# Where the GLA's low-rank decay keeps its temporaries: arena slots, or the mLSTM's second state tile and the LRU weights' tile

## The chip, the cores and the metric

One core of one Trainium2 chip runs the whole program once per launch. The metric is device microseconds per execution. Five engines work beside each other, each in its own order: TensorE (PE, with its weight loads PEld), VectorE (DVE), ScalarE (ACT), GpSimd (POOL) and SyncE (SP), which issues the DMAs. All data is float32; a matmul with float32 accuracy is made of three passes over operands that were split into a high and a low part.

## The reference, cut to what matters

One decoder layer over 2048 tokens of width 1024: a norm, one input projection, four token mixers side by side (RG-LRU, mLSTM, HGRN2, GLA), each times a gate path and projected, merged by sigmoid gates, and an output projection. HGRN2 and GLA are the same recurrence with different decays:

```python
def step(state, xs):                      # gla_chunkwise, per chunk
    G = jnp.cumsum(gc, axis=2)
    diff = jnp.where(mask[:, :, None], G[:, :, :, None, :] - G[:, :, None, :, :], -jnp.inf)
    A = jnp.einsum('bhtd,bhsd,bhtsd->bhts', qc, kc, jnp.exp(diff))
    o = jnp.einsum('bhts,bhse->bhte', A, vc) + jnp.einsum('bhtd,bhde->bhte', qc * jnp.exp(G), state)
    ...
log_gk = jax.nn.log_sigmoid(g_lr @ g_w_lr2 + g_b_lr2) / GLA_GATE_TAU     # the low-rank decay, rank 16
og = gla_chunkwise(q, k, v, log_gk)
merged = jnp.sum(gates * proj, axis=2)    # four branches, in the order lru, mlstm, hgrn2, gla
```

## The kernel before, in words

The sequence is worked off in two halves of 1024 tokens; everything below happens once per half. Channels lie on the partitions, tokens on the free axis, in pieces of 512.

`ahead_pairs` makes most of the input projection, the LRU and the mLSTM. The mLSTM keeps its state in two tiles `self.C[0]` and `self.C[1]` (trace name `Cst`), read and written in turn; `self.lw` holds the LRU's block weights. Then comes `mixers`:

- `ip_vals(0..3)` makes the values of HGRN2 (0, 1) and GLA (2, 3) with TensorE; calls 2 and 3 also give the 16 columns `lrt` from which the decay is made (L1152, L1154, L1156 empty PSUM). Matmuls are line L284.
- Six rounds, called round 0 to round 5 here, of two `gla_tile`s each: round 0 and 1 are HGRN2 heads 0 and 1 (first and second 512 tokens), 2 and 3 are heads 2 and 3, 4 and 5 are the GLA's two pairs of heads. Each tile goes through a chain of small steps: scans L994 and L996 (from L995), exponents L999 to L1001, products L1002 and L1003, 32-wide matmuls L1019, four refinements L1038 to L1062, state and outputs L1075 to L1111, a norm L1121 to L1134, and a store of its output `y`.
- `load(r + 1)` loads the next round's inputs. In program order round 1 comes after `ip_vals(2)`, `ip_vals(3)`, `gla_decay()` and `load(2)`.
- `gla_decay` (L1189 to L1216) transposes `lrt` into `lt` (L1199, L1200), multiplies by the low-rank weights (L1206) and makes four decay tiles `g` of 512 tokens, each with one temporary `t`: Identity, Abs, Exp (L1208 to L1210), Ln (L231), then L1212 and L1213 on DVE. The decays are first read in rounds 4 and 5.
- `gates_ahead` makes the last six merge gates (matmuls L272).

`merge` then runs the four branches' projections (L272 again, 192 matmuls of 512 columns per branch) and multiplies each by its gate (L1331). Branches one and two take four fixed buffers (the two `gth` tiles and the two halves of `lw`), branches three and four take arena slots. Branch three needs rounds 0 to 3, branch four rounds 4 and 5.

Order of the work: the program is traced in order, then a scheduler places every instruction on its engine by a simulated timeline, the one with the lowest priority number first among those whose operands are ready. `mix()` lowers the number of `gla_decay` and of the tiles by 4000. So a later part may run ahead of an earlier one, unless it writes memory that the earlier one has still to read.

That memory is the `Arena`: 46 slots in `mixers`, 0 to 21 named `arena` in the trace, 22 to 29 `ma`, 30 to 45 `mb`. `get` takes the next free slot after the last one taken, and wraps; free and taken are counted in program order. At the start of `gla_decay` the turn stands at slot 22. With 27, 29 and 0 to 3 in use it gives: `lt` 22 and 23; `g` 24, 25 with `t` 26, 28; `g` 4, 5 with `t` 6, 7. `load(2)` gets 8 to 13, 22 and 23. Round 1 gets, first tile: `Gc` 26, `g8` 28, `d` 30, `wq` 31, `wk` 32; second tile: `Gc` 35, `g8` 36, `d` 37, `wq` 6, `wk` 7.

Of the kernel before, what the change touches and what calls it, by code (L numbers as in the profile page):

```python
# [145 lines left out]
class Trunk:  # L146
# [1043 lines left out]
    def gla_decay(self):  # L1190

        nc = self.nc
        V, A, T = nc.vector, nc.scalar, nc.tensor
        gs = []
        lt = self.F()
        for n in range(2):
            ps = self.pbank()
            for c in range(4):
                T.transpose(ps[0:16, c * 128:(c + 1) * 128], self.lrt[:, n * 4 + c, :], self.cs("id"))  # L1199
            V.tensor_copy(lt[0:16, n * 512:(n + 1) * 512], ps[0:16])  # L1200
        for p in range(2):
            gs.append([self.T(0, NU + 2 * NA if p else None) for _ in range(2)])
            for n in range(2):
                g, t = gs[p][n], self.T()
                ps = self.pbank()
                T.matmul(ps, self.wlr[:, p * 128:(p + 1) * 128], lt[0:16, n * 512:(n + 1) * 512], start=True, stop=True)  # L1206
                gg, tt = g[:, :512], t[:, :512]
                A.activation(gg, ps, AF.Identity, bias=self.pv("gb", p))  # L1208
                A.activation(tt, gg, AF.Abs)
                A.activation(tt, tt, AF.Exp, scale=-1.0)  # L1210
                self.ln(tt, tt, bias=1.0)
                V.scalar_tensor_tensor(gg, gg, 0.0, tt, op0=ALU.min, op1=ALU.subtract)  # L1212
                V.tensor_scalar(gg, gg, 1.0 / 16, None, op0=ALU.mult)  # L1213
                self.free(t)
        self.free(lt)
        return gs  # L1216


# [342 lines left out]
```

## Time and profile before

| | us |
|---|---|
| median of 3 runs (2855.47 to 2863.75) | 2856.83 |
| profiled execution | 2859.04 |
| its span from first to last instruction | 2857.0 |
| PE busy / weight loads busy | 2603.6 / 2149.5 |
| DVE, POOL, ACT busy | 1780.5, 1528.5, 1327.9 |

Busy times are averages over very different stages, so the stretches below are read one by one. "PEclk" is the TensorE clock that was granted, as a share of full speed. In a timeline the bracket at the end of a row is the engine's idle time before that row and what ended it.

### The profile page before, as it was taken

Reading aid. Unit: us, or ns where it says so; the run is one execution under the profiler, and the core shown is the slowest. Engines: PE = TensorE matmul, PEld = TensorE weight load, DVE = VectorE, ACT = ScalarE, POOL = GpSimd, SP = SyncE. Lnnn points to the kernel's source line nnn. Section 1 sums busy time; section 2 is a strip of 40 time slices with the busy share of each in tenths; the row PEclk is TensorE's granted clock in tenths of the full one; section 3 lists DMA queues with packets and bytes.
Section 4 is the critical chain, followed back from the end, with each engine's and each line's share of the span. In section 5 each row is a group of like instructions: output and inputs, shape, how many; then the busy total and the mean of one; then the engine's idle time right before and its main releaser. Section 6 shows DMA issues by size and latency. Waiting matters only on the chain. (4 is left out here: it accounts for less than half of the span.)

```text
span 2857.0 us, 45749 instructions
## 1 busy us (share of the span) xinstructions
PE 2603.6 (91%) x16800; PEld 2149.5 (75%) x16800; DVE 1780.5 (62%) x2907; ACT 1327.9 (46%) x2793; POOL 1528.5 (53%) x1273
## 2 busy tenths in 40 slices
PE   6999999999999977859999999997999998888699
PEld 4778778778889765648977778885888896676489
DVE  7686776877662777523476957757766618775241
ACT  5355444644432545562454445456344325445523
POOL 5566555444462766346475566553444627645563
PEclk9999999999999988779999999998999998989799
DMA  5133224454542465454432333244454424546631
GB/s 209 67 132 109 92 85 145 133 174 144 149 144 75 130 207 168 175 204 149 146 133 78 136 108 107 89 133 144 153 155 126 156 70 144 195 153 211 202 100 71
DMA packets 227071, 393.02 MB, mean 138 GB/s; under 512 B 20720, under 2 KB 78080, under 8 KB 226848
## 3 DMA queue, kind: packets, MB, share of 16 engines
q1 hardware_dynamic: 226848, 390.11, 41.4%
q8 instruction: 132, 2.16, 0.3%
q14 instruction: 91, 0.75, 0.1%
HBM read 270.42 MB, written 119.60 MB: 137 GB/s over the span
## 5 line engine op out<-in xcount | busy, mean ns | idle before, releaser
L422 POOL TENSOR_TENSOR wl<-wr,wh 128x512 fp32r<-128x512 f32 x264 | 370.4, 1408 | 314.4 <-ACT wh L421 285.9
L422 POOL TENSOR_TENSOR wl<-gth,wh 128x512 fp32r<-128x512 f32 x198 | 287.8, 1454 | 296.7 <-ACT wh L421 272.9
L254 POOL TENSOR_TENSOR wl<-wr,wh 128x512 fp32r<-128x512 f32 (+1 forms) x176 | 252.9, 1447 | 260.6 <-ACT wh L253 247.7
L427 PE MATMUL mx<-s,wh 128*128 128x512 f32 x1104 | 355.2, 400 | 19.9 <-POOL s L310 12.0
L272 PE MATMUL pb<-hh,wh 128*128 128x512 f32 x704 | 303.1, 432 | 38.3 <-DVE arena L1331 18.6
L427 PE MATMUL mx<-hh,wl 128*128 128x512 f32 x776 | 309.4, 399 | 6.4 <-POOL wl L422 6.4
L427 PE MATMUL mx<-hh,wh 128*128 128x512 f32 x776 | 308.8, 398 | 3.9 <-ACT wh L421 3.9
L427 PE MATMUL mx<-hl,wh 128*128 128x512 f32 x776 | 308.4, 397 | 0.0
L436 DVE TENSOR_TENSOR arena<-arena,mx 128x512 f32<-128x512 f32 x348 | 228.4, 680 | 121.6 <-PE mx L427 112.0
L272 PE MATMUL pb<-hl,wh 128*128 128x512 f32 x704 | 297.1, 422 | 2.5 <-DVE hl L1305 2.5
L272 PE MATMUL pb<-hh,wl 128*128 128x512 f32 x704 | 295.6, 420 | 0.0
L421 ACT ACTIVATE wh<-wr 128x512 fp32r<-128x512 f32 x264 | 164.1, 625 | 216.2 <-PE mx L427 126.5
L427 PEld LDWEIGHTS mx<-s,wh 128*128 128x128 f32 x1104 | 208.5, 190 | 73.5 <-POOL s L310 13.3
L284 PE MATMUL pb<-wl,hh 128*128 128x256 f32 (+1 forms) x880 | 250.5, 285 | 0.5 <-POOL wl L254 0.5
L284 PE MATMUL pb<-wh,hh 128*128 128x256 f32 (+1 forms) x880 | 249.8, 285 | 1.0 <-DVE ob L1366 1.0
L284 PE MATMUL pb<-wh,hl 128*128 128x256 f32 (+1 forms) x880 | 249.8, 284 | 0.0
L421 ACT ACTIVATE wh<-gth 128x512 fp32r<-128x512 f32 x198 | 124.1, 627 | 240.3 <-DVE gth L432 181.5
L427 PE MATMUL mx<-s,wl 128*128 128x512 f32 x552 | 218.0, 398 | 0.0
L272 PEld LDWEIGHTS pb<-hh,wh 128*128 128x128 f32 x704 | 143.3, 204 | 80.2 <-DVE arena L1331 20.4
L253 ACT ACTIVATE wh<-wr 128x512 fp32r<-128x512 f32 (+1 forms) x176 | 110.2, 628 | 151.2 <-PE pb L272 95.2
L427 PEld LDWEIGHTS mx<-hh,wl 128*128 128x128 f32 x776 | 146.7, 189 | 44.4 <-POOL wl L422 11.4
L427 PEld LDWEIGHTS mx<-hh,wh 128*128 128x128 f32 x776 | 147.4, 190 | 39.7 <-ACT wh L421 5.2
(535 smaller groups left out, 6338.5 us busy)
## 6 DMA issues: line engine op xcount, KB each, us to landing
wr<-in_wc_dram SPq DMA_DIRECT2D x246, 256.0 KB, 2.8
g<-arena SPq DMA_DIRECT2D x52, 512.0 KB, 3.9
gth<-in_wc_dram SPq DMA_DIRECT2D x66, 256.0 KB, 2.7
wr<-in_wb_dram SPq DMA_DIRECT2D x64, 256.0 KB, 3.5
hl<-y SPq DMA_DIRECT2D x32, 512.0 KB, 6.1
arena<-g SPq DMA_DIRECT2D x56, 256.0 KB, 3.3
y<-arena SPq DMA_DIRECT2D x36, 256.0 KB, 3.9
arena<-in_xT_dram SPq DMA_DIRECT2D x32, 256.0 KB, 5.1
```

Of the source, the lines that this page charges most:

```text
L253: nc.scalar.activation(hi, raw, AF.Copy)
L254: nc.gpsimd.tensor_tensor(lo, raw, hi, op=ALU.subtract)
L272: nc.tensor.matmul(ps, w[:, ws], h[:, ts], start=(k == 0 and i == 0), stop=(k == nk - 1 and i == 2))
L284: self.nc.tensor.matmul(v, h[:, cs], w[:, ws], start=(first and i == 0), stop=(last and i == 2))
L421: A.activation(hi, w, AF.Copy)
L422: G.tensor_tensor(lo, w, hi, op=ALU.subtract)
L427: nc.tensor.matmul(ps, wp[:, ws], xp, start=(k == 0 and i == 0), stop=(k == 3 and i == 2))
L436: V.tensor_tensor(o, x, y, op=ALU.add)
```

## The change

`gla_decay` no longer takes slots for `lt` and `t`. `lt` becomes the first 16 partitions of `self.lw`, and all four chains share the first 512 columns of `self.C[1]` as their one temporary. The four `g` still come from the arena.

```diff
-        lt = self.F()
+        lt = self.lw.rearrange("p a b -> p (a b)")
...
-                g, t = gs[p][n], self.T()
+                g = gs[p][n]
...
-                gg, tt = g[:, :512], t[:, :512]
+                gg, tt = g[:, :512], self.C[1][:, :512]
...
-                self.free(t)
-        self.free(lt)
         return gs
```

## Rows read from the trace of the kernel before

**Rows 1.** The page: busy time, share of the span and instructions of each engine.

```profile
PE 2603.6 (91%) x16800; PEld 2149.5 (75%) x16800; DVE 1780.5 (62%) x2907; ACT 1327.9 (46%) x2793; POOL 1528.5 (53%) x1273
```

**Rows 2.** Busy us per stretch, first half: PE, PEld, DVE, ACT, POOL; PEclk, DMA share, GB/s.

```profile
825.00:876.00 51.00, 46.17 (x574) 44.61 (x573) 37.12 (x62) 21.96 (x60) 30.95 (x32) 0.97 0.34 116
...
880.00:935.00 55.00, 54.58 (x448) 53.63 (x446) 7.81 (x36) 12.54 (x30) 14.25 (x12) 1.00 0.16 44
935.00:1003.00 68.00, 58.52 (x512) 45.74 (x510) 52.84 (x71) 39.97 (x92) 51.04 (x48) 0.92 0.47 152
1003.00:1060.00 57.00, 47.55 (x402) 37.56 (x402) 42.34 (x69) 27.05 (x64) 33.83 (x35) 0.85 0.60 206
1060.00:1119.00 59.00, 48.35 (x494) 37.69 (x494) 43.34 (x80) 31.62 (x69) 40.17 (x41) 0.91 0.46 143
1119.00:1189.00 70.00, 53.22 (x699) 41.89 (x698) 37.66 (x70) 40.01 (x98) 24.46 (x28) 0.77 0.42 139
1189.00:1264.00 75.00, 49.80 (x617) 38.70 (x616) 30.28 (x64) 39.50 (x99) 35.09 (x36) 0.76 0.63 222
```

**Rows 3.** The same view, second half.

```profile
2243.00:2294.00 51.00, 45.02 (x564) 43.42 (x563) 36.95 (x62) 21.97 (x60) 30.93 (x32) 0.97 0.33 112
...
2298.00:2353.00 55.00, 54.58 (x449) 53.82 (x448) 7.62 (x36) 12.54 (x30) 14.32 (x12) 1.00 0.15 43
2353.00:2425.00 72.00, 63.19 (x576) 47.89 (x574) 55.41 (x73) 39.55 (x91) 55.12 (x50) 0.88 0.41 135
...
2595.00:2672.00 77.00, 50.10 (x570) 38.37 (x570) 31.11 (x65) 44.12 (x107) 36.95 (x37) 0.79 0.65 223
```

**Rows 4.** DVE's timeline: the output step that ends rounds 0, 1 and 5.

```profile
875.60 0.69 DVE L1134 TENSOR_TENSOR mb<-mx,mb 128x512 f32<-128x512 f32 x1 [0.20 <-PE mx L1133]
...
1002.82 0.68 DVE L1134 TENSOR_TENSOR arena<-mx,arena 128x512 f32<-128x512 f32 x1
...
1264.30 0.69 DVE L1134 TENSOR_TENSOR arena<-mx,arena 128x512 f32<-128x512 f32 x1 [1.17 <-PE mx L1133]
```

**Rows 5.** ACT's timeline: the exponent of round 1's second tile, both halves.

```profile
951.49 0.63 ACT L1001 ACTIVATE arena<-mb 128x512 f32<-128x512 f32 x1 [2.88 <-DVE arena L1212]
...
2369.25 0.63 ACT L1001 ACTIVATE arena<-mb 128x512 f32<-128x512 f32 x1 [1.94 <-DVE arena L1212]
```

**Rows 6.** DVE's timeline around the decay: L1212 of the decay, L994 of round 1.

```profile
939.58 0.69 DVE L1212 SCALAR_TENSOR_TENSOR ma<-ma,ma 128x512 f32<-128x512 f32 x1 [4.46 <-ACT ma L231]
...
940.65 1.63 DVE L994 TENSOR_TENSOR_SCAN ma<-cst,mb 128x512 f32<-128x512 f32 x1
...
949.93 1.52 DVE L1212 SCALAR_TENSOR_TENSOR arena<-arena 128x512 f32<-128x512 f32 x1
```

**Rows 7.** POOL's timelines: round 1's second tile before the decay, both halves.

```profile
879.45 1.04 POOL L999 TENSOR_TENSOR mb<-mb 128x512 f32<-128x512 f32 x1 [4.17 <-DMA y<-mb]
...
2297.73 1.04 POOL L999 TENSOR_TENSOR mb<-mb 128x512 f32<-128x512 f32 x1 [4.55 <-DMA y<-mb]
```

**Rows 8.** L272 alone per stretch: PE busy, PEld busy (instructions); PEclk, DMA, GB/s.

```profile
935.00:1003.00 68.00, 45.08 (x168) 32.85 (x168) 0.92 0.47 152
1003.00:1264.00 261.00, 132.22 (x432) 90.97 (x432) 0.82 0.53 178
1264.00:1362.00 98.00, 81.78 (x336) 64.32 (x336) 0.93 0.53 172
```

**Rows 9.** DVE's timeline: the last gate product of branch two, and of branch four.

```profile
1207.83 0.67 DVE L1331 SCALAR_TENSOR_TENSOR gth<-gth,pb 128x512 f32<-128x512 f32 x1
1361.56 0.67 DVE L1331 SCALAR_TENSOR_TENSOR arena<-arena,pb 128x512 f32<-128x512 f32 x1
2627.83 0.68 DVE L1331 SCALAR_TENSOR_TENSOR gth<-gth,pb 128x512 f32<-128x512 f32 x1
2766.29 0.68 DVE L1331 SCALAR_TENSOR_TENSOR arena<-arena,pb 128x512 f32<-128x512 f32 x1
```

**Rows 10.** The chain that ended last: its longest piece (start, us, what).

```profile
2684.95 61.52 PE pb L272 x264
```

## The prediction

> **What bounds the kernel now.** Over the whole span PE is busy 91% [rows 1], but that is an average. Read the stretches of the first half next [rows 2]; their edges are the ends of the GLA rounds, taken from the output step L1134 [rows 4]. Three things are to be seen. From 880 to 935 PE works without a gap on `ip_vals(2)` and `(3)` (54.6 of 55 us, clock 1.00), while DVE is busy 7.8 us, ACT 12.5, POOL 14.3: the vector engines have almost nothing to do, although round 0 is over and round 1's inputs are there. From 935 to 1264 the picture turns: rounds 1 to 5 take 68, 57, 59, 70 and 75 us, and PE idles in each (9.5, 9.5, 10.7, 16.8, 25.2 us; the sum is 72) at a clock of 0.92 down to 0.76. After 1264 PE runs nearly through: 336 matmuls of L272 in 98 us [rows 8]. The second half shows the same [rows 3]. So in this part of each half the time is set by how soon round 5 is over and how much of PE's merge work is left then.
>
> Why does round 1 not use the 55 us before it? Its second tile got as far as L999 at 879.45 and 2297.73 [rows 7]. Its next steps write `wq` and `wk`, slots 6 and 7, and stand until the decay's L1212 has read its temporary out of those slots: L1001 comes at 951.49 and 2369.25, each time released by L1212 [rows 5]. The first tile scans into slot 26, the first chain's `t`: its L994 comes at 940.65, right behind the L1212 of 939.58 [rows 6]. The decay itself needs the last column of `ip_vals(3)`. Both tiles of round 1 thus wait for 55 us of PE work which they don't need, through four slots.
>
> **The change, part by part.**
>
> *Slots.* Followed through the allocator's rule, six takings fall out and every later one shifts. `g` gets 22 to 25, `load(2)` 26, 28 and 30 to 35, round 1 gets 36, 37, 4, 5, 6 (first tile) and 9, 10, 11, 12, 13 (second). Their last owners are all of round 0; the last to be released are the gate path of its second tile (slot 37, free when `y` has landed) and its last temporaries. Rows 7 show that moment, the wait for `DMA y<-mb`: 879.45 and 2297.73. So round 1 can run from 880 and 2298, under `ip_vals`.
>
> *Round 1's length there.* Nearest row: round 0, which ran under `ip_vals(1)` in 51 us in both halves [rows 2, 3]. Farthest: round 1 beside the gates, 68 and 72 us. I take 55, nearer to round 0 since PE's other work is of the same kind. Round 1 ends at 935 instead of 1003, and at 2353 instead of 2425: 68 and 72 us earlier (bounds 51 and 55; 72 and 76).
>
> *Rounds 2 to 5.* Among themselves their slots keep the same owners up to round 4, so they follow round 1 as before. The same gates and branches one and two now lie beside four rounds instead of five; I put 8 us on that (between 0 and the 16 us by which round 1 beside the gates was longer than round 0). Round 5 ends at 1264 - 68 + 8 = 1204, and at 2672 - 72 + 8 = 2608.
>
> *PE's stream.* Round 1's PE work moves ahead of the gates: 58.5 - 45.1 for L272 [rows 2, 8], less some 4.7 for the decay, is 8.7 us, plus the idle time that such a round brings (51 - 46.2 = 4.8, round 0): 13.5 us. The gates, and branches one and two behind them, come 13.5 us later: the last gate product of branch two at 1208 + 13.5 = 1222 and 2628 + 13.5 = 2642 [rows 9]. Then branches three and four follow without a hole, since round 5 is over: 384 matmuls at 61.52/264 = 0.233 us [rows 10] are 89 us, and 2 us for the last product. Ends: 1313 against 1362, and 2733 against 2766 [rows 9]: 49 + 33 = 82 us gained, if branches one and two keep their old pace (32 products in 185 us, 5.8 each). With round 5 gone at 1204 and 2608, the last 18 and 34 us of them run alone; at the pace of branch four (2.8 each, 12 matmuls) they would take half as long, 9 + 17 = 26 us more gained. I take half of that: 95 us.
>
> *The third branch's buffers.* Now 432 - 384 = 48 of its matmuls run before round 5 is over [rows 8], as their first buffers lie on slots 0 and 4, inputs that round 5 is soon done with. The turn then stands at 15: the first buffers fall on 15, 17, 19 and 21, the values that round 5 reads to its end. Those 48, 11.2 us, move behind round 5; the 384 above already hold them.
>
> *One temporary for four chains.* Abs, Exp and Ln of a chain wait until L1212 of the chain before has read. From L1212 at 939.58 to the last at 949.93 the four chains now take 10.4 us with DVE's scans between them [rows 6]; in series some 12 to 16 (three ACT steps of 0.63 and an L1212 of 0.7 to 1.5 each, plus waits). First reader is round 4, over 100 us later: nothing, as long as round 1 no longer stands behind it. `lw` and `C[1]` have no other user there: the mLSTM is over, the LRU too, and the first merge buffer in `lw` comes after the gates.
>
> *Sum.* 2859 - 95 = 2764 for the profiled execution, which lies 2 us above the median of the runs: **2762**. From below: round 1 at 51 us, no loss in the others, the stream never late: 72 + 76 = 148 us, less the 22 us of third-branch work that moves behind round 5, is 126, or 2731; and fewer gaps may win back some clock (432 matmuls of L272 took 132 us at 0.82 [rows 8], 101 at 0.233), for which I go 9 us further, to 2722. From above: round 1 takes 68 to 72 us and the stream keeps its pace: 2775.
>
> **The rivals.**
>
> *The interleaving costs PE its clock (2809).* Round 1's 32-column matmuls cut into `ip_vals`. For: rounds 4 and 5, with many small matmuls and gaps, were granted 0.77 and 0.76 [rows 2], a good part of them at 1.2 instead of 2.4 GHz. Against: round 0 under `ip_vals(1)` was granted 0.97 in both halves. At 0.77 the 54.6 us become 70.9, the stream starts 30 instead of 13.5 us late: 1330 and 2750, 32 + 16 = 48 us gained. The Trainium skill ("Perfetto Trace Analysis", section Matmul Optimizations) says that the engine scales its power with its use and that matmuls should therefore run back to back in batches; by that rule, this is what happens. Round 0's 0.97 speaks against it here.
>
> *Round 1 doesn't move (2857).* If something besides the four slots holds it, the decay's place ahead of it in program order for instance, only the order shifts a little. Against: its second tile did run ahead to L999 [rows 7].
>
> *Slower: the third branch is starved (2879).* If round 1 doesn't move, the buffers do: the 48 matmuls lie behind round 5 in each half, 2 x 11.2 us on the path. It decides as soon as round 5's end moves up by less than 11 us per half.
>
> **How the numbers follow.** Forecast, 2722 to 2775 with 2762 as the likeliest: 0.72. Half the gain or less but over 0.3% (the clock's rival, or rounds 2 to 5 stretched by the denser work), 2775 to 2848: 0.16. No move: 0.06. Slower: 0.06. A measurement of this kernel can tell about 0.3% from no change, 8.6 us. Faster 0.88, same 0.06, slower 0.06. The range must leave out no more than 0.2: 2722 to 2832 reaches over the clock's rival to a gain of 25 us.
>
> **What would show it.** Right: between 880 and 935 (2298 and 2353) DVE's busy time rises from 8 to over 30 us, L1134 of round 1 comes before or about the decay's L1212; L994 of round 1 isn't released by L1212; PE idles less than 15 us between the end of round 4 and that of branch three. The last L272 before round 5's end belongs to branch two. Wrong: round 1 still starts after the decay (then the slots were not what held it); a granted clock under 0.9 in those 55 us (the clock's rival); rounds 2 to 5 longer by as much as round 1 has gained, with DVE near 90% in them (then DVE is the bound, and the slots only moved the wait); or branches one and two ending as late as before although the rounds end 60 us earlier (then the merge's four buffers are the bound).

## The result, and the profile after

| | before | after |
|---|---|---|
| median of 4 runs each (us) | 2856.15 (2855.29 to 2863.75) | 2775.62 (2774.05 to 2778.96) |
| span of the profiled execution (us) | 2857.0 | 2777.2 |
| PE / DVE / POOL / ACT busy (us) | 2603.6 / 1780.5 / 1528.5 / 1327.9 | 2597.5 / 1776.6 / 1534.9 / 1310.8 |

The ratio is 0.9714, with an interval of 0.9695 to 0.9733: 80.5 us off, where 95 were forecast (2762), inside the range of 2722 to 2832. The engines do the same work as before; what went is time in which PE stood still, 2857.0 - 2603.6 = 253 us before, 2777.2 - 2597.5 = 180 after.

From line 1215 on, lines of the kernel after stand two lower (L1331 of before is L1329, the gate's tanh L1321 is L1319). The busy times by stretch, the columns as in [rows 2]: the edges are the ends of rounds 0 to 3, of rounds 4 and 5, of branch two and of branch four.

```profile
868.00:924.00 56.00, 49.85 (x687) 46.46 (x686) 46.30 (x85) 27.30 (x73) 45.40 (x47) 0.98 0.20 63
924.00:961.00 37.00, 37.00 (x404) 35.48 (x403) 23.25 (x62) 17.17 (x56) 16.43 (x19) 0.95 0.32 101
961.00:1028.00 67.00, 58.22 (x645) 44.53 (x645) 57.69 (x85) 42.18 (x96) 60.23 (x57) 0.89 0.26 80
...
1082.00:1142.00 60.00, 51.21 (x694) 40.84 (x680) 29.55 (x66) 31.90 (x90) 16.31 (x23) 0.86 0.58 191
1142.00:1211.00 69.00, 59.66 (x238) 46.41 (x236) 18.36 (x24) 26.52 (x40) 28.63 (x22) 0.93 1.00 360
1211.00:1304.00 93.00, 92.39 (x423) 76.05 (x424) 38.79 (x50) 25.80 (x42) 68.48 (x51) 1.00 0.52 162
```

The same view, second half.

```profile
2246.00:2301.00 55.00, 50.14 (x696) 46.82 (x695) 46.14 (x85) 27.63 (x75) 45.26 (x47) 1.00 0.21 64
...
2532.00:2592.00 60.00, 52.53 (x211) 41.24 (x210) 17.25 (x22) 23.56 (x36) 25.59 (x21) 0.94 0.98 358
2592.00:2686.00 94.00, 94.00 (x430) 77.31 (x430) 38.45 (x49) 27.90 (x45) 70.50 (x53) 1.00 0.40 128
```

In the first line of each half DVE is busy 46 us of 56 and of 55, where the stretch after round 0 had 8 of 55 [rows 2, 3]: round 1 is in it, and PE keeps its clock (0.98 and 1.00). Round 2 follows under `ip_vals` too (37 us, PE without a gap). Then the picture is another than before: round 5 is over at 1142, and it is PE's stream, branches one and two, that goes on until 1211, with DMA at 1.00 and 360 GB/s. From there on PE runs through.

The places of the single steps, in DVE's timeline (start, duration, engine, line; in brackets the idle time before it and what ended it): ends of rounds 0, 1 and 5 (L1134), first and last decay (L1212), last gate product of branch two and of branch four (L1329), then the same of the second half.

```profile
868.09 0.69 DVE L1134 TENSOR_TENSOR mb<-mx,mb 128x512 f32<-128x512 f32 x1 [1.41 <-PE mx L1133]
924.38 0.67 DVE L1134 TENSOR_TENSOR mb<-mx,mb 128x512 f32<-128x512 f32 x1
972.82 1.78 DVE L1212 SCALAR_TENSOR_TENSOR ma<-ma,Cst 128x512 f32<-128x512 f32 x1
990.10 0.69 DVE L1212 SCALAR_TENSOR_TENSOR ma<-ma,Cst 128x512 f32<-128x512 f32 x1 [0.54 <-ACT Cst L231]
1141.29 1.47 DVE L1134 TENSOR_TENSOR arena<-mx,arena 128x512 f32<-128x512 f32 x2
1211.38 0.68 DVE L1329 SCALAR_TENSOR_TENSOR gth<-gth,pb 128x512 f32<-128x512 f32 x1
1303.74 0.69 DVE L1329 SCALAR_TENSOR_TENSOR arena<-arena,pb 128x512 f32<-128x512 f32 x1
...
2246.32 0.69 DVE L1134 TENSOR_TENSOR mb<-mx,mb 128x512 f32<-128x512 f32 x1 [1.41 <-PE mx L1133]
2301.27 0.68 DVE L1134 TENSOR_TENSOR mb<-mx,mb 128x512 f32<-128x512 f32 x1
2532.38 0.69 DVE L1134 TENSOR_TENSOR arena<-mx,arena 128x512 f32<-128x512 f32 x1 [1.44 <-PE mx L1133]
2592.04 0.69 DVE L1329 SCALAR_TENSOR_TENSOR gth<-gth,pb 128x512 f32<-128x512 f32 x1 [0.85 <-ACT gth L1319]
2686.49 0.67 DVE L1329 SCALAR_TENSOR_TENSOR arena<-arena,pb 128x512 f32<-128x512 f32 x1
```

Round 1's exponents, the first two rows of ACT's timeline, come 105 and 94 us before the first decay. The first is no longer released by L1212 [rows 5] but by L1133 of round 0: by the allocator's rule round 1's second tile writes slot 13 here, and L1133 is the last reader of what lay in it. The next two rows are already round 2's, by the rule on slots 29 (`ma`) and 8; they too come before the first decay, by 64 and 57 us:

```profile
868.09 0.64 ACT L1001 ACTIVATE arena<-arena 128x512 f32<-128x512 f32 x1 [2.20 <-PE mx L1133]
...
878.58 0.62 ACT L1001 ACTIVATE arena<-arena 128x512 f32<-128x512 f32 x1
...
909.30 0.63 ACT L1001 ACTIVATE ma<-arena 128x512 f32<-128x512 f32 x1 [3.10 <-POOL arena L999]
...
915.78 0.65 ACT L1001 ACTIVATE arena<-arena 128x512 f32<-128x512 f32 x1
```

The four chains through one temporary do run in series. The last one's Abs waits for the reader of the third, and first to last L1212 is 990.1 - 972.8 = 17.3 us, against 949.9 - 939.6 = 10.3 before [rows 6]:

```profile
985.64 0.63 ACT L1209 ACTIVATE Cst<-ma 128x512 f32<-128x512 f32 x1 [2.73 <-DVE ma L1212]
```

For all that follows, each half is measured from its own end of round 0, since runs differ by some us before it. After / before, first and second half: round 1 ends at 56, 55 / 127, 131; round 5 at 274, 286 / 389, 379; branch two's last product comes at 343, 346 / 332, 333; branch four's at 436, 440 / 486, 472. So the halves gain 50 + 32 = 82 us. Round 0 ended 7.5 us earlier in this execution, and from branch four to the next round 0 it took 942 us instead of 932; 82 + 7.5 - 10 = 79.5 is the difference of the spans (79.8). The order of the work is the same in both kernels up to some 830 us, and there the kernel after is already 5 us ahead, so most of the 7.5 us lie between runs (round 0 ends at 867 to 876 us in all the kernels here, and at 873 in the second profile of the kernel after, e11). The 10 us may be partly the change's: where the stream of gates ends late that stretch is 935 to 943 us long, in the others 931 to 937, and once 945. Why stays open.

### The profile page after: what moved, and what is told of

Same layout as the page of the kernel before. It is cut to its first block, busy times and chain, and to the rows that moved or that the text cites. A ratio compares the mean times of both kernels' runs of the same rounds, so it can differ in the third digit from the quotient of the medians.

```text
span 2777.2 us, 45729 instructions
## 1 busy us (share of the span) xinstructions
PE 2597.5 (94%) x16800; PEld 2151.9 (77%) x16800; DVE 1776.6 (64%) x2907; ACT 1310.8 (47%) x2779; POOL 1534.9 (55%) x1273
## 5 line engine op out<-in xcount | busy, mean ns | idle before, releaser
L272 PE MATMUL pb<-hh,wh 128*128 128x512 f32 x704 | 294.5, 419 | 25.3 <-DVE lw L1329 15.2
L272 PE MATMUL pb<-hl,wh 128*128 128x512 f32 x704 | 291.6, 414 | 0.0
L272 PE MATMUL pb<-hh,wl 128*128 128x512 f32 x704 | 289.3, 411 | 0.0
L284 PE MATMUL pb<-wl,hh 128*128 128x256 f32 (+1 forms) x880 | 255.8, 291 | 3.3 <-POOL wl L254 3.3
L284 PE MATMUL pb<-wh,hh 128*128 128x256 f32 (+1 forms) x880 | 256.4, 292 | 1.6 <-ACT arena L1077 0.9
L284 PE MATMUL pb<-wh,hl 128*128 128x256 f32 (+1 forms) x880 | 254.5, 290 | 0.0
L272 PEld LDWEIGHTS pb<-hh,wh 128*128 128x128 f32 x704 | 140.3, 199 | 66.9 <-DVE lw L1329 18.5
```

What stands on the lines that cost most here:

```text
L272: nc.tensor.matmul(ps, w[:, ws], h[:, ts], start=(k == 0 and i == 0), stop=(k == nk - 1 and i == 2))
L284: self.nc.tensor.matmul(v, h[:, cs], w[:, ws], start=(first and i == 0), stop=(last and i == 2))
```

## The experiments

The question was which of two things gave the gain, since the change does two: it takes away **the wait** of round 1 for the decay, and by leaving out six takings it shifts **the turn of the slots** for everything behind it. And what sets the end now? All times are medians; the columns are us from the end of round 0, first and second half, read from L1134 and the gate product as above; "R" is a round, "b2" and "b4" the last products of branches two and four.

| kernel | R1 ends | R5 ends | b2 | b4 | time, us | ratio to before (95%) |
|---|---|---|---|---|---|---|
| before | 127, 131 | 389, 379 | 332, 333 | 486, 472 | 2856.15 | 1 |
| after | 56, 55 | 274, 286 | 343, 346 | 436, 440 | 2775.62 | 0.9714 (0.9695 to 0.9733) |
| e1: wait gone, old turn | 43, 45 | 270, 286 | 348, 346 | 442, 440 | 2781.77 | 0.9727 (0.9683 to 0.9770) |
| e2: wait kept, new turn | 133, 135 | 352, 357 | 333, 321 | 448, 443 | 2783.09 | 0.9732 (0.9682 to 0.9781) |
| e3: round 2 waits | 48, 47 | 342, 346 | 365, 356 | 459, 454 | 2808.45 | 0.9822 (0.9778 to 0.9865) |
| e4: `t` alone moved | 111, 114 | 361, 354 | 336, 310 | 457, 450 | 2807.50 | 0.9812 (0.9769 to 0.9854) |
| e5: `lt` alone moved | 123, 123 | 364, 358 | 318, 319 | 450, 445 | 2790.04 | 0.9783 (0.9761 to 0.9804) |
| e6: before, two tiles off the store | 128, 130 | 368, 359 | 324, 320 | 460, 456 | 2812.59 | 0.9851 (0.9831 to 0.9870) |
| e10: before, three tiles | 129, 136 | 363, 356 | 323, 330 | 458, 449 | 2811.77 | 0.9851 (0.9830 to 0.9872) |
| e8: after, half of branch one | 58, 55 | 286, 281 | 326, 328 | 419, 424 | 2746.95 | 0.9619 (0.9599 to 0.9638) |
| e9: before, half of branch one | 127, 132 | 379, 378 | 271, 294 | 477, 472 | 2850.57 | 0.9981 (0.9961 to 1.0001) |
| e7: after, fifth buffer | 56, 55 | 274, 283 | 336, 340 | 430, 433 | 2766.53 | 0.9691 (0.9670 to 0.9712) |
| e11: after again | 56, 56 | 273, 283 | 341, 342 | 434, 436 | 2773.73 | 0.9728 (0.9709 to 0.9747) |
| e12: fifth buffer again | 56, 55 | 271, 281 | 333, 338 | 427, 431 | 2767.07 | 0.9695 (0.9674 to 0.9715) |

One regularity runs through all 28 halves: b4 lies 85 to 98 us behind the **later** of R5 and b2. Two streams meet at the third branch: the chain of rounds, and PE's stream of gates and branches one and two. In before, e2, e4, e5, e6, e9 and e10 the chain comes last, in after, e1, e3, e7, e8, e11 and e12 the stream. The experiments are read with this rule. It is a description of these halves, good to some 12 us, and no more.

**The wait and the turn apart (e1, e2).** e1 is the kernel after, but takes the six slots again and leaves them unused; e2 has the new turn, but puts the temporaries back on slots that round 1 takes next.

```diff
 e1, on after
+        keep = self.F()
...
-                g = gs[p][n]
+                g, t = gs[p][n], self.T()
...
+                self.free(t)
+        self.free(keep)
```

> The changed kernel, but the six slots of the decay's temporaries are still taken and given back in the arena, unused: every later buffer lies where it lay before the change, and no wait for the decay's temporaries is left. Theory W (the gain is the wait that went): as the changed kernel, 2776 us, or up to 22 us less because the third branch's first buffers lie as before (2754 to 2776); round 1 ends near 924. Theory R (the gain is the other place of the later buffers): as before, 2856 us.

```diff
 e2, on after (slot(u, k) names the arena's slots u to u + k - 1)
-        lt = self.lw.rearrange("p a b -> p (a b)")
+        lt = self.slot(34, 2)
...
-                gg, tt = g[:, :512], self.C[1][:, :512]
+                gg, tt = g[:, :512], self.slot((36, 37, 12, 13)[2 * p + n])[:, :512]
```

> The changed kernel's places for all later buffers, but the decay's temporaries lie in the slots that round 1 (36, 37, 12, 13) and load(2) (34, 35) take next, so the waits of before are back. Theory W: as before or slower, 2856 us, up to 2879 if the third branch's buffers cost the 22 us that the prediction put on them. Theory R: as the changed kernel, 2776 us.

e1 came out as the kernel after, as theory W (the wait) has it: 6 us above W's range, but the two ratios cannot be told apart. e2 did not: W wanted 2856 or more, measured were 2783. And yet the wait is back in it, as ACT's timeline shows (L1216 is the decay's L1212 there), and round 1 ends as late as before:

```profile
943.11 0.63 ACT L1001 ACTIVATE arena<-arena 128x512 f32<-128x512 f32 x1 [2.23 <-DVE ma L1216]
```

DVE's timeline of e2, ends of round 1 and round 5:

```profile
999.26 0.68 DVE L1134 TENSOR_TENSOR mb<-mx,mb 128x512 f32<-128x512 f32 x1
...
1218.50 0.68 DVE L1134 TENSOR_TENSOR arena<-mx,arena 128x512 f32<-128x512 f32 x1
```

From the end of round 1 to that of round 5 it takes 219 and 222 us in e2, 261 and 248 in before. Against the runs of before on the same chip (2858.36) e1 gains 77 us and e2 75; both parts together gain 80. They don't add because of the rule above: with the wait gone round 5 ends at 274, but then the stream, at 343, is later, and what the chain gains beyond that is worth nothing.

**Only part of the way (e3, e4, e5).** In e3 round 1 is free, and round 2 meets the decay's slots. e4 and e5 are the kernel before with one of the two tiles moved.

```diff
 e3, on after
+        lt = self.slot(30, 2)
...
+                gg, tt = g[:, :512], (self.C[1] if p or n else self.slot(34))[:, :512]
 e4, on before
-                g, t = gs[p][n], self.T()
+                g = gs[p][n]
...
-                gg, tt = g[:, :512], t[:, :512]
+                gg, tt = g[:, :512], self.C[1][:, :512]
...
-                self.free(t)
 e5, on before
-        lt = self.F()
+        lt = self.lw.rearrange("p a b -> p (a b)")
...
-        self.free(lt)
```

> The changed kernel with the low-rank tile in slots 30 and 31 and the first chain's temporary in slot 34: round 1 is free, round 2's first inputs wait for the decay again. Theory S (PE's stream of gates and branches sets the end): within 12 us of the changed kernel, 2764 to 2788. Theory C (the chain of rounds sets the end): rounds 3 to 5 end some 37 us later in each half, 2850 us.

> Half of the change: the chains' temporary is the state tile, the low-rank tile stays in the arena. Its slots 22 and 23 are the next ones of round 1's second tile (its two weighted products), so that tile still waits for the decay's last matmul and its first tile is free. Theory W: between the two kernels, 2790 to 2845 us. Theory S: if PE's stream sets the end and only the last matmul of the decay is waited for, nearer to the changed kernel, below 2800.

> One half of the change alone: lt in the LRU weights' tile, the four temporaries t still from the arena. By the allocator's rule the turn then gives round 1's first tile slots that the decay has not had (6 to 13), its second tile slots 24, 25, 30 and 31, three of the four temporaries among them; round 2's second tile lies on round 1's inputs again, and round 4's first tile on both gate paths of round 3. Theory W+D (round 1 waits for the decay, later rounds for the store before them): round 1 still ends at 985 to 1003 us, rounds 2 and 4 stay as long as in the kernel before, round 5 is 5 to 10 us shorter, 2832 to 2852 us. Rival H (each half of the change gives about half of its gain): 2805 to 2825 us.

e3 fits neither of its theories. Its stream is the later one (b2 at 365 and 356), but 22 and 11 us later than in the kernel after. Here are the stretches from the end of round 0 to b2, both halves of e3 and then of the kernel after:

```profile
869.00:1233.50 364.50, 303.13 (x3168) 249.70 (x3167) 210.45 (x381) 184.13 (x447) 191.97 (x188) 0.87 0.49 164
2269.50:2626.00 356.50, 296.98 (x3164) 244.57 (x3164) 207.76 (x382) 180.80 (x445) 184.46 (x187) 0.89 0.49 164
...
869.00:1211.50 342.50, 303.29 (x3172) 248.72 (x3171) 209.15 (x382) 180.53 (x445) 194.85 (x188) 0.92 0.53 178
2247.00:2592.50 345.50, 300.15 (x3167) 248.06 (x3167) 209.58 (x382) 183.29 (x447) 193.33 (x188) 0.91 0.50 172
```

PE does the same work in both (303 and 297 us busy against 303 and 300), and stands still for 61 and 60 us instead of 39 and 45. In e3 only round 1 lies under `ip_vals`, in after round 2 as well; that the waiting comes from this is argued. So S was right that the stream sets the end, and wrong that its length is fixed. e4 lies where W put it, within wide bounds: round 1 is 16 and 17 us shorter, not 71 and 76, since by the allocator's rule its second tile gets `lt`'s slots.

e5 was faster than both of its theories had it. Round 1 ends late (994 and 2375) and round 2 is as long as before (57 us in both halves, before 57 and 55), as W+D said. Round 5 is hardly shorter (76 and 75 us, before 75 and 78), and round 4 is (54 and 52 us instead of 70 and 58), although by the allocator's rule its first tile lies on two gate paths; so that part of W+D fell. A term that neither theory had shows in the tail: b4 comes 85 and 87 us after round 5, not 97 and 94. L272 alone between these two points, in e5:

```profile
1235.00:1321.00 86.00, 75.05 (x312) 59.57 (x312) 0.98 0.54 162
```

312 matmuls where before had 336 [rows 8]: 24 fewer are left for PE when round 5 is over, at 0.233 us [rows 10] 5.6 us of PE. Of a half's 64 gate products 37 lie ahead of round 5's end, in before 34. That fits the prediction's paragraph on the third branch's buffers, with the other sign: by the allocator's rule the turn stands at 28 when the merge begins in e5, and the first buffers fall on 28, 0, 2 and 4. That these come free early enough is argued, not measured.

**What the old turn cost (e6, e10).** By the allocator's rule `d` of round 2's second tile and `wk` of round 4's second tile lay on slots 3 and 35, gate paths of the round before, which come free only when `y` has been stored from them. e6 is the kernel before with just these two in the scratch tile `self.C[1]`; the slots stay taken, and `d0` and `wk0` are given back in their place, so nothing else shifts. e10 also moves `Gc` of round 5's first tile (slot 9).

```diff
 e6, on before
+        d0, wk0 = d, wk
+        if gi == 0 and js == [3]:
+            d = self.C[1]
+        if gi == 0 and js == [2, 3]:
+            wk = self.C[1]
...
 e10, besides
+        Gc0 = Gc
+        if gi == 1 and js == [0, 1]:
+            Gc = self.C[1]
...
```

> The kernel before with two tiles of the rounds moved, and nothing else: d of round 2's second tile and wk of round 4's second tile lie in the state's scratch tile instead of their arena slots (which stay taken, so that every other tile keeps its slot). In the kernel before these two slots held the gate path of the round before, and come free only when its y has been stored. Theory D (what the change's new turn of the slots took out of rounds 2 to 5 is this wait for the store): round 2 lasts some 45 us instead of 57, round 4 some 55 instead of 70, round 5 ends 20 to 27 us earlier in each half, and since the chain of rounds sets the end there, 2805 to 2817 us. Rival N (the rounds became shorter for another reason, such as the streams of weights or the decay's own place): 2850 to 2860 us, rounds 2 and 4 as long as before.

> The kernel before with three tiles of the rounds in the state's scratch tile, one after the other: the two of the experiment before (d of round 2's second tile, wk of round 4's second tile) and Gc of round 5's first tile, which lay on the gate path of round 4's second tile. Theory D (the store of y holds the next round wherever a tile of it lies on the gate path): L994 of round 5's first tile waits for no store of y, round 5 lasts 66 to 70 us instead of 75 to 78, and the whole takes 2793 to 2803 us. Rival N (round 5 is as long for another reason, its products or the stores of the merge): 2808 to 2815 us, as with two tiles moved.

e6 came out as theory D has it, 2812.59. The exponent that writes `wk` in round 4, in ACT's timeline of before:

```profile
1127.68 0.62 ACT L1001 ACTIVATE mb<-mb 128x512 f32<-128x512 f32 x1
```

and the same step in e6 (L1006 there), into the scratch tile:

```profile
1087.75 0.62 ACT L1006 ACTIVATE Cst<-mb 128x512 f32<-128x512 f32 x1
```

It starts 40 us earlier, of which 7 are the earlier round 0. Rounds 2 to 5 take 241 and 229 us instead of 261 and 248: 21 and 19 us less, of 42 and 26 that the whole new turn gave in e2. This much of the turn's gain is shown to be the store of `y`. The single rounds fit D less well: round 2 takes 53 and 45 us and round 4 60 and 57 (before 57 and 55, 70 and 58), and round 3 is shorter too, by 6 and 8. The new turn is not free of such tiles either: by the allocator's rule `wk` of round 4's second tile and of round 5's first lie on slots 45 and 12 there, gate paths of the round before. What counts is thus which step of a round meets the store, and when. The third tile is a different matter. In e6 the scan of round 5's first tile still waits for the store:

```profile
1172.14 1.23 DVE L994 TENSOR_TENSOR_SCAN arena<-cst,ma 128x512 f32<-128x512 f32 x1 [2.14 <-DMA y<-arena]
```

In e10 (L997) it doesn't, and runs 69 us ahead of that:

```profile
1103.61 1.21 DVE L997 TENSOR_TENSOR_SCAN Cst<-cst,ma 128x512 f32<-128x512 f32 x1
```

Round 5 is shorter for it, 66 and 65 us about as D said, but round 4 is 3 and 4 us longer, and the time is that of e6 within 1 us, as N said. In the profiled executions b4 comes 2 and 8 us earlier than in e6, and 5 us of that go again between the halves. With intervals of some 5 us to either side of each ratio, a gain of a few us cannot be excluded; the 10 to 20 us that D expected did not come. In the second half the three tiles reach e2's 222 us (e10: 220); in the first, 15 us of the turn's gain (234 against 219) stay unexplained.

**What sets the end (e8, e9).** Both leave out half of branch one's products, e8 in the kernel after, e9 in the kernel before.

```diff
+        nk = nk or 4 * len(pieces)
...
-                self.proj_ch(self.wpieces([self.a["wb"][n, j]]), *bufs[ni], add)
+                self.proj_ch(self.wpieces([self.a["wb"][n, j]]), *bufs[ni], add, nk=2 if ni == 0 else None)
```

> The kernel after, in which branch one's projection leaves out half of its products: 96 matmuls fewer in each half, 22 us of TensorE at the full clock; all transfers stay. Theory S (after the change TensorE's stream through branches one and two sets the end): branch four ends 15 to 22 us earlier in each half until the chain of rounds takes over, 2732 to 2750 us. Rival C (the chain of rounds still sets the end after the change): 2770 to 2780 us. Rival D (the stream is bound by its transfers or its buffers, not by TensorE's work): 2765 to 2776 us.

> The kernel before, in which branch one's projection leaves out half of its products: 96 matmuls fewer in each half, 22 us of TensorE at the full clock; all transfers stay. Theory C (before the change the chain of rounds sets the end, and what TensorE has less to do is lost in waiting): 2848 to 2858 us, with round 5 ending where it did, 1264 and 2672 us. Rival S (TensorE's stream sets the end there too): 2812 to 2825 us.

The same cut of 44 us of PE's work takes 29 us off the kernel after, and from the kernel before no more than can be told from nothing (0.9981, with 1.0001 in the interval). In e9 branches one and two end 61 and 39 us earlier, round 5 only 9 and 1 us; the gap between them is filled with waiting. Busy time in e9 from branch two's last product to the end of round 5:

```profile
1142.00:1250.00 108.00, 56.53 (x779) 44.84 (x775) 41.03 (x84) 63.91 (x169) 42.52 (x44) 0.67 0.43 147
```

PE is busy about half of it, at a granted clock of 0.67. The chain of rounds sets the pace there. In e8 b2 and b4 both come 16 to 18 us earlier in each half, and round 5 (286, 281) is still far ahead of b2: the stream sets the end, and most of the 22 us of PE's work that were left out lay on its path.

**The stream's buffers (e7, e11, e12).** The chain of the kernel after shows another part of the stream. Some of its pieces (start, us, what) between round 5's end and branch two's:

```profile
2533.00 4.71 DMA gth<-g
2537.72 0.76 SPq L1317
...
2538.57 7.94 DMA hl<-y
2546.53 5.81 DMA lw<-g
...
2552.43 0.70 DVE lw L1329
...
2553.17 4.43 PE pb L272 x12
```

By the kernel's order a gate's load into `gth` or `lw` can start only when the product before it in that buffer is stored. e7 gives branches one and two a fifth buffer, the scratch tile `C[1]`; e12 is the same kernel and e11 the kernel after, run side by side.

```diff
+        own.append(self.C[1][:, :512])
...
-            return own[self.gt % 4]
+            return own[self.gt % 5]
```

> The kernel after with a fifth buffer for the gates of branches one and two, in the state's scratch tile, which nothing else needs by then. Theory B (in the kernel after the end is set by TensorE's stream of gates and branches, and this stream is held by the round trip of its four buffers): branch two's last product comes 5 to 10 us earlier in each half, 2755 to 2766 us. Rival T (the stream is bound by TensorE's own work and by the weights' transfers, whose DMA share is 0.99 in 1143 to 1212 us): 2772 to 2780 us, and branch two's last product within 3 us of its place.

> The kernel after once more, unchanged, beside the next one on the same chip: 2770 to 2781 us by its earlier runs.

> The kernel after with the fifth buffer once more, beside the kernel after on the same chip. Theory B (the fifth buffer takes 6 to 7 us out of branches one and two in each half): 8 to 14 us below the kernel after. Rival T (the first difference of 9 us was one between runs): within 4 us of it.

The last product of branch two is now made in the fifth buffer, in e12 at 1203.82 + 0.69 against 1214.43 + 0.68 in e11 (DVE's timelines):

```profile
1203.82 0.69 DVE L1330 SCALAR_TENSOR_TENSOR Cst<-Cst,pb 128x512 f32<-128x512 f32 x1 [1.95 <-ACT Cst L1320]
```

```profile
1214.43 0.68 DVE L1329 SCALAR_TENSOR_TENSOR gth<-gth,pb 128x512 f32<-128x512 f32 x1
```

From round 0's end that is 7 to 8 us less in the first half and 4 to 6 in the second. The times of e12 and e11 lie 6.7 us apart, 2760.67 to 2768.58 and 2770.70 to 2777.71, which do not overlap; e7 was 9.1 us below the first result of after. The gain is real but smaller than the 8 to 14 us expected; the intervals of the two ratios still touch. Of the kernels here that do the whole work, this one (e7, e12) is the fastest.

## Why the prediction came out as it did

*Round 1 is held by four slots, and runs at 880 and 2298 once they are free.* Right. It was put at 55 us long from the end of round 0 and took 56 and 55; PE kept 0.98 and 1.00 of its clock, and the **clock's rival** is out. The Trainium skill ("Perfetto Trace Analysis", section Matmul Optimizations) asks for matmuls in batches, back to back. Here small ones between large ones cost little that can be seen: PE was busy 50 of 56 and 50 of 55 us.

*The third branch starved, round 1 not moving.* Neither happened. The third branch's products did all move behind round 5, and the stream before them hid it.

*Rounds 2 to 5 keep the same owners and follow 8 us slower.* This step failed. They took 218 and 231 us from the end of round 1 instead of 261 and 248, for two reasons that the prediction missed. Six takings fewer shift every later tile, and in the old turn tiles of rounds 2 and 4 lay on the gate paths of the round before (e6: some 20 us per half). And round 2 as well as round 1 went under `ip_vals`, where it takes 37 and 41 us. e1 and e2 have one reason each: with the old turn and round 1 free, rounds 2 to 5 take 227 and 241 us, with the new turn and round 1 held 219 and 222. So once round 1 is free the new turn is worth only 10 us more per half. The turn was followed through round 1 with care and taken for granted behind it. e2 shows the price of that: with the wait of round 1 left in place, the turn alone gives 0.9732.

*PE's stream comes 13.5 us later, branches one and two keep their pace or win 13 us.* The end of the stream was right: b2 was expected 346 and 348 us after round 0 at the old pace, and came at 343 and 346. The way there was not. The last matmul of `ip_vals` (L284) starts at 965.66 and 2346.79, 97 and 100 us behind round 0 where before it was 56 in both halves, since round 2 lies in it as well, and the 32 products of branches one and two then took 141 and 143 us instead of 185 and 178. The two errors cancel: round 2's work, too, moved ahead of the gates and was missing beside the branches. That it came out within 3 us is in part luck, for in e3 the same work of PE ended 22 and 11 us later, with more waiting in it.

*The signs.* Two of those named for being right did not come. PE idled 18.7 and 23.5 us between the end of round 4 and that of branch three, not under 15, and round 5 ended with 13 and 14 gate products done, so beside branch one (its first 16) and not branch two: it was over 69 and 60 us before b2, where 18 and 34 were forecast. One of those named for being wrong did come: branches one and two ended as late as before, indeed 10 and 12 us later, while round 5 ended 115 and 93 us earlier. It could not tell right from wrong, since the forecast itself had b2 13.5 us later. Its reading, that the four buffers are the bound, holds in part only: a fifth buffer gave 4 to 8 us per half (e7, e12), leaving out 22 us of PE's work 16 to 18 (e8).

*95 us.* At the old pace the sum was 82, and 82 is what the halves gained. The 13 us on top, for the last products running without the rounds beside them, were mis-sized. The products did run faster, 44 and 35 us for the 32 of a half, but the first of them came 55 and 48 us later than before, not 13.5, and that took it back. Nor did they reach branch four's pace: from 1142 to 1211 19 products took 69 us, 3.6 each and not 2.8. DMA is busy 1.00 there, at 360 GB/s, where 162 flow beside branch four; that this is why is argued. The Trainium skill ("Perfetto Trace Analysis", section Engine Utilization) gives 358 GB/s as a core's share of the memory bandwidth when both cores of a pair draw on it, and lets one that is active alone go to some 120% of that. The trace agrees: 360 over the whole stretch, and for 20 us of the second half 402:

```profile
2580.00:2600.00 20.00, 17.36 (x74) 13.85 (x75) 9.10 (x10) 10.04 (x15) 12.12 (x9) 1.00 1.04 402
```

e7 and e8 show that buffers and PE's work have their share in the pace too.

*The decay in series, 12 to 16 us, costs nothing.* It took 17.3 us. The first readers are not over 100 us later, as the prediction had it, but close behind: the first scans of round 4's two tiles (L994), which read the first and the third decay, ready at 975.8 and 986.1 (ends of L1213):

```profile
986.26 1.21 DVE L994 TENSOR_TENSOR_SCAN mb<-cst,ma 128x512 f32<-128x512 f32 x1
...
1008.57 1.21 DVE L994 TENSOR_TENSOR_SCAN mb<-cst,ma 128x512 f32<-128x512 f32 x1
```

That is 10 and 22 us to spare. That the series costs nothing is argued from this distance; no run took it away by itself.

*Was it room that was lacking?* The Trainium skill ("Perfetto Trace Analysis", section Optimization Strategy) reads a gap that repeats as a sign that there may not be enough memory for the next tile. That is not the case here: e1 takes as many slots as the kernel before, and is as fast as the kernel after within the intervals. What counts is whose slot comes next, not how many there are.

## What to carry to other kernels

Where tiles are taken in turn from shared memory, leaving a taking out moves every tile behind it: follow the turn to the end of the loop, and look above all for tiles that fall on something that is still to be stored. Where two streams meet, work out both ends before adding gains up: each of two repairs of the slower stream may give nearly the whole, and both together hardly more, as here 77, 75 and 80 us. A wait that vanishes from the trace is worth only what the next one leaves: the third tile of e10 started 69 us earlier, and the medians differ by 1 us.

## What the runs showed of the hardware that was not expected

PE took a whole round's small matmuls between `ip_vals`' large ones at a granted clock of 0.98 and 1.00, busy 50 of 56 and 50 of 55 us. Only at the end of the first of these stretches did the clock fall to its lower level, 1.2 GHz (0.50), with PE busy 48 of the 53.5 us before:

```profile
868.00:921.50 53.50, 47.95 (x649) 44.62 (x647) 43.80 (x79) 26.14 (x71) 43.12 (x44) 1.00 0.20 61
921.50:928.00 6.50, 5.90 (x87) 5.42 (x88) 6.44 (x19) 2.62 (x6) 3.38 (x6) 0.50 0.24 84
```

The same kind of work with more waiting was granted 0.76 (PE busy 50 of 75 us [rows 2]) and, in e9, 0.67 (57 of 108). In these rows a low clock goes with the waiting beside the work, not with the size of the matmuls; no run separates the two further.
